# Input norms of the MLP and the conv folded into the norm that follows, squares of x summed later, small adds moved from GpSimd to VectorE

## The chip, the cores and the metric

The kernel runs on one core of a Trainium2 chip. The metric is the time of one execution in microseconds (us); the time of a version is the median of its runs. Engines are named as in the profile: PE is TensorE, DVE VectorE, ACT ScalarE, POOL GpSimd, SP SyncE.

## The reference

512 tokens of 1024 features pass through two layers of a first block, an mLSTM layer and a short-convolution layer, each followed by an MLP, and then through a second block (attention and a mixture of experts), which the change does not touch. Each mixer and each MLP stands between two RMS norms: one of its input, one of its output.

```python
def rms_norm(x, g):
    y = xf * lax.rsqrt(jnp.mean(xf * xf, axis=-1, keepdims=True) + EPS)
    return y * g

def short_conv_mixer(x, w_in, w_conv, w_out):
    bgate, cgate, xh = jnp.split(x @ w_in, 3, axis=-1)
    u = cgate * xh
    conv = lax.conv_general_dilated(u, w_conv[:, None, :], padding=[(CONV_WIDTH - 1, 0)],
                                    feature_group_count=D_MODEL, ...)
    return (bgate * conv) @ w_out

def sqrelu_mlp(x, w_up, w_down):
    h = jax.nn.relu(x @ w_up)
    return (h * h) @ w_down

for i in range(2):
    h = rms_norm(x, g[0])
    h = mlstm_mixer(h, ...) if i == 0 else short_conv_mixer(h, ...)
    x = x + rms_norm(h, g[1])
    h = sqrelu_mlp(rms_norm(x, g[2]), w_mlp_up[i], w_mlp_down[i])
    x = x + rms_norm(h, g[3])
```

Since relu is homogeneous, the factor rstd(x) of the norm in front of an MLP can be applied to the MLP's operand, to its hidden values (once, before the square) or to its output (as a square). In the conv it enters three times, once in each of bgate, cgate and xh.

## The kernel before

Everything is kept with features on the partitions and tokens along the free dimension, in eight feature tiles of 128 x 512 (`xres` is x). A float32 product is three matmuls on parts split into a high and a low part: `mm3` issues lines 92, 93 and 94. Weights come by DMA into `raw`; `wpiece` splits them: ACT casts the high part `wh` (line 85), another engine subtracts for the low part `wl` (line 86, on DVE unless `eng` says otherwise).

A layer ends in `boundary`. The last products of the layer come in four parts for each half of the tokens (256 each). `evac` takes them out of PSUM into `y` and gives their squares to `Sumsq.add` (ACT squares, line 194; the adds on line 196, on POOL except for the last two tiles). `colsum` sums these over the partitions by PE (line 207) and `rstd_cols` makes rstd(y) of it on DVE and ACT (lines 156 to 162); `bcast_rows` spreads it as a row over all partitions by PE transposes (line 216). Then `residual` handles feature tile after feature tile:

```python
nc.vector.scalar_tensor_tensor(t, self.y[k][:, sl], self.gpost(k), self.rb, ...)         # line 281
nc.vector.tensor_add(xk, xk, t)                                                          # 286: x += t
nc.scalar.activation(h, xk, AF.Copy, scale=self.gnext(k))                                # 288: high part
nc.vector.scalar_tensor_tensor(lo, xk, self.gnext(k), h.bitcast(F32), ...)               # 289: low part
nc.scalar.activation(self.sq[k][:, sl], xk, AF.Square)                                   # 292
```

`h` and `lo` are the operand (`op`) of the first products of the next layer, which `first` issues for the weight pieces w0 and w1, first with half 0 of the tokens, then with half 1. `squares` adds the squares of x (line 297, on POOL). A last column sum gives rstd(x), which the next layer gets as a function that makes rows of it (`rows`): the input norm is not applied to the operand, but to what comes out of the first products: in `mlp` at line 611 together with the relu, in `conv` at lines 713, 714 and 722. There are three such layer changes, mLSTM to MLP, MLP to conv, and conv to MLP; the second MLP ends in `boundary_out`, which feeds the attention instead.

`mlp` runs over eight blocks of 512 hidden features: up-products, `act` (relu, square, split), and `down`, whose results stay in `y`. At the first block they are copied there by ACT (line 660), later added by DVE (line 662), and the last block ends in the boundary. Between blocks a `filler` runs that prepares the second block's modulation vectors; its products on PE are line 816.

Each engine runs its instructions in the order in which they stand in its program; a scheduler in the building of the program moves some of them.

Of the kernel before, what the change touches and what calls it, by code (L numbers as in the profile page):

```python
# [18 lines left out]
S = 512  # L19
# [8 lines left out]
class Net:  # L28
# [123 lines left out]
    def rstd_cols(self, ms, w, scale):  # L152
        """(ms * scale + eps) ** -0.5 on [128, w]: a seed from a logarithm, one Newton step"""
# [21 lines left out]
    class Sumsq:  # L175
        """sums of squares over feature tiles, [128, S]"""
# [6 lines left out]
        def add(self, src, sl=slice(0, S)):  # L183
# [19 lines left out]
    def colsum(self, acc, d=D, n=4):  # L203
# [4 lines left out]
        return self.rstd_cols(pc[:, :n], n, 1.0 / d), pc  # L208
# [14 lines left out]
    def load_x(self, w):  # L223
        """x and the first weights, in the order of their use"""
# [10 lines left out]
    def start(self, first):  # L235
        """x feature-major, its split, first(k, operand) after each, then the statistics"""
# [19 lines left out]
    class Boundary:  # L256
        """The last products of one layer (mm(half, part), evac(half, part) for four parts finish y and ss) and the
        residual x += y * rstd(y) * gpost, one half of the tokens after the other."""

        def __init__(self, net, mm, evac, y, ss, gpost, gnext=None):  # L260
            self.net, self.mm, self.evac, self.y, self.ss, self.gpost, self.gnext = net, mm, evac, y, ss, gpost, gnext
            self.sq = [None] * KD
            self.ops = [(net.t([128, S], F32R, tag="op"), net.t([128, S], F32R, tag="op")) for _ in range(KD)] if gnext else None
            self.acc = net.t([128, S], tag="acc")
# [5 lines left out]
        def colsum(self, hf):  # L270
            self.c = self.net.colsum(self.ss.acc[:, self.net.HALF[hf]], n=2)
# [4 lines left out]
        def residual(self, hf, ks):  # L276
            net, nc = self.net, self.net.nc
            sl = net.HALF[hf]
            for k in ks:
# [5 lines left out]
                else:  # L285
# [20 lines left out]
    def boundary(self, mm, evac, y, ss, gpost, gnext, wnext):  # L306
        """... and the first products of the next layer; returns its operand, these products, a function for rows of rstd(x)"""
        b = self.Boundary(self, mm, evac, y, ss, gpost, gnext)
# [12 lines left out]
        w1 = self.wpiece(wnext[1], KD, 256, eng=self.nc.gpsimd)  # L321
# [3 lines left out]
        b.squares(0)  # L325
# [10 lines left out]
    def boundary_out(self, mm, evac, y, ss, gpost, fill):  # L336
        """... other products filling in; returns columns of rstd(x) for each half"""
        b = self.Boundary(self, mm, evac, y, ss, gpost)
# [29 lines left out]
    def mlstm(self):  # L368
# [87 lines left out]
        def stage_a(h):  # L456
            """what needs queries, keys and gates only"""
# [26 lines left out]
        def tokmajor(c0, act):  # L484
            """a token-major 256 column piece; act(chunk, psum)"""
# [83 lines left out]
    def out_proj(self, w, ops, gpost, gnext, wnext):  # L569
        """x += rmsnorm(w^T ops); returns the next operand"""  # L570
# [27 lines left out]
        return self.boundary(mm, evac, y, ss, gpost, gnext, wnext)  # L598

    def mlp(self, l, ops, pu0, rows, gpost, gnext, wnext, filler, fill=None):  # L600
# [8 lines left out]
        def act(u, src):  # L609
            t = self.t([128, S])  # L610
# [1093 lines left out]
```

## Time and profile before

| | |
|---|---|
| runs | 1860.73, 1858.69 and 1860.83 us; median 1860.73 |
| span of the profiled execution | 1854.4 us from the first to the last instruction |
| PE | 96% busy, mean granted clock 0.982 |
| DVE | 57% |
| ACT | 34% |
| POOL | 13% |
| DMA | 133 GB/s read from HBM, on average |

The profile was taken of one execution, and no time of its own is given for it beside the span: the median of the runs is 6.3 us longer than the span. The span ends at the last instruction that the profile shows. The granted clock is a share of TensorE's full speed of 2.4 GHz; 0.50 is the lower level of 1.2 GHz. A stretch with a share between the two has seen both.

### The profile page before, as it was taken

What the parts mean: (1) busy time and instruction counts of PE and PEld (TensorE: products, weight loads), DVE (VectorE), ACT (ScalarE), POOL (GpSimd) and SP (SyncE); (2) the same over time, 40 slices, a digit from 0 to 9 for tenths busy, and PEclk for the clock granted to TensorE, in tenths of its full rate; (3) what the DMA queues carried; (4) which work ended last, traced back from release to release, by engine and by line L of the source; (5) the groups of instructions that cost most, each with busy time, mean ns of one, the idle gap of its engine ahead of it and who ended that gap; (6) DMA issues with size and microseconds to landing.
All of it is one profiled execution on the core that took longest, in us unless ns stands there. A gap on an engine that the chain in (4) does not pass through costs nothing.

```text
span 1854.4 us, 24565 instructions
## 1 busy us (share of the span) xinstructions
PE 1774.5 (96%) x9877; PEld 1405.3 (76%) x9881; DVE 1059.3 (57%) x1935; ACT 635.0 (34%) x1150; POOL 238.8 (13%) x213
## 2 busy tenths in 40 slices
PE   7999999999999899999999999989989997999997
PEld 5799888888888888888888888888777886454534
DVE  4644674777765665746556445677777744132322
ACT  4444453222222432244322222344656633111112
POOL 1000140000000422222000001113233322000000
PEclk9999999999999899999999999989999998999999
DMA  6222423444542222532443332220100066799992
GB/s 191 69 69 69 159 69 114 133 133 134 178 141 97 72 69 93 162 109 92 136 136 95 102 103 91 69 73 12 24 13 16 13 202 226 257 387 386 387 373 103
DMA packets 191809, 248.19 MB, mean 134 GB/s; under 512 B 19783, under 2 KB 125648, under 8 KB 191568
## 3 DMA queue, kind: packets, MB, share of 16 engines
q1 hardware_dynamic: 188688, 244.70, 39.3%
q10 hardware_dynamic: 2656, 1.87, 0.3%
q8 instruction: 77, 1.26, 0.3%
q14 instruction: 36, 0.29, 0.1%
q0 software_dynamic: 352, 0.06, 0.0%
HBM read 244.52 MB, written 2.10 MB: 133 GB/s over the span
## 4 chain that ended last, share of the span: by engine, by line
PE 85%; DVE 9%; ACT 3%; issue 1%; POOL 1%; DMA 0%; SPq 0%; DVEq 0%; ACTq 0%; POOLq 0%
PE ps L92 21%; PE ps L93 20%; PE ps L94 20%; PE ps L1515 6%; PE ps L1489 3%; PE ps L1468 2%; PE ps L1115 2%; PE ps L1100 2%; DVE op L289 1%; DVE th L281 1%; DVE wl L86 1%; DVE xres L286 1%; PE pw L1243 1%; PE ps L1481 1%; PE ps L1482 1%
## 5 line engine op out<-in xcount | busy, mean ns | idle before, releaser
L93 PE MATMUL ps<-op,wh 128*128 128x512 f32 (+1 forms) x1808 | 663.8, 368 | 13.8 <-DVE op L289 13.1
L92 PE MATMUL ps<-op,wh 128*128 128x512 f32 (+1 forms) x1808 | 661.5, 370 | 8.4 <-ACT wh L85 2.9
L94 PE MATMUL ps<-op,wl 128*128 128x512 f32 (+1 forms) x1808 | 660.5, 367 | 0.0
L93 PEld LDWEIGHTS ps<-op,wh 128*128 128x128 f32 x1808 | 345.9, 192 | 75.9 <-DVE op L289 16.3
L92 PEld LDWEIGHTS ps<-op,wh 128*128 128x128 f32 x1808 | 343.3, 192 | 69.4 <-ACT op L288 4.1
L94 PEld LDWEIGHTS ps<-op,wl 128*128 128x128 f32 x1808 | 345.5, 191 | 59.2
L86 DVE TENSOR_TENSOR wl<-raw,wh 128x1024 fp32r<-128x1024 f32 x204 | 254.7, 1253 | 208.0 <-ACT wh L85 206.5
L85 ACT CAST wh<-raw 128x1024 fp32r<-128x1024 f32 x210 | 219.7, 1052 | 405.3 <-PE ps L93 284.6
L662 DVE TENSOR_TENSOR t<-t,ps 128x512 f32<-128x512 f32 x96 | 65.8, 686 | 110.1 <-PE ps L94 110.0
L1515 PE MATMUL ps<-mw,xs 128*64 128x512 f32 x400 | 107.1, 602 | 0.0
L811 DVE SCALAR_TENSOR_TENSOR u<-b,csilu,u 128x256 f32<-128x256 f32 x224 | 97.7, 479 | 4.4 <-DMA b<-in_w_mod_dram 3.5
L613 ACT ACTIVATE t<-t 128x512 f32<-128x512 f32 x64 | 40.3, 630 | 146.3 <-DVE t L611 146.0
L92 PE MATMUL ps<-wh,op 128*128 128x256 f32 x256 | 74.8, 293 | 0.1
L1499 DVE SCALAR_TENSOR_TENSOR ys<-ps,sm,ys 128x512 fp32r<-128x512 f32 x14 | 10.5, 749 | 110.0 <-ACT ys L1498 110.0
L93 PE MATMUL ps<-wl,op 128*128 128x256 f32 x256 | 72.0, 282 | 0.0
L94 PE MATMUL ps<-wh,op 128*128 128x256 f32 x256 | 71.5, 284 | 0.0
L611 DVE SCALAR_TENSOR_TENSOR t<-ps,rb 128x512 f32<-128x512 f32 x64 | 43.9, 688 | 47.7 <-PE ps L94 47.7
L1068 DVE TENSOR_REDUCE sm<-pw 128x1 f32<-128x768 f32 (+2 forms) x64 | 53.9, 854 | 30.0 <-PE pw L1243 17.4
L1515 PEld LDWEIGHTS ps<-mw,xs 128*64 128x64 f32 x400 | 31.3, 137 | 52.2 <-issue 49.9
L92 PEld LDWEIGHTS ps<-wh,op 128*128 128x128 f32 x256 | 48.2, 188 | 4.1 <-ACT og L507 2.3
L93 PEld LDWEIGHTS ps<-wl,op 128*128 128x128 f32 x256 | 48.3, 189 | 0.2
L94 PEld LDWEIGHTS ps<-wh,op 128*128 128x128 f32 x256 | 47.5, 188 | 0.1
(460 smaller groups left out, 2409.5 us busy)
## 6 DMA issues: line engine op xcount, KB each, us to landing
raw<-in_w_mlp_up_dram SPq DMA_DIRECT2D x32, 1024.0 KB, 5.4
raw<-in_w_mlp_down_dram SPq DMA_DIRECT2D x32, 1024.0 KB, 5.0
mw<-in_w_gate_dram SPq DMA_DIRECT2D x26, 1024.0 KB, 14.1
b<-in_w_mod_dram SPq DMA_DIRECT2D x48, 512.0 KB, 4.2
mw<-in_w_up_dram SPq DMA_DIRECT2D x24, 1024.0 KB, 14.2
mw<-in_w_down_dram SPq DMA_DIRECT2D x17, 1024.0 KB, 14.4
raw<-in_w_in_conv_dram SPq DMA_DIRECT2D x12, 1024.0 KB, 5.1
raw<-in_w_in_mlstm_dram SPq DMA_DIRECT2D x11, 1024.0 KB, 5.4
```

The costliest lines, as they stand in the source:

```text
L85: nc.scalar.copy(h, raw[:, k0:k0 + kk])
L86: (eng or nc.vector).tensor_sub(lo, raw[:, k0:k0 + kk], h.bitcast(F32))
L92: mm(out, st[0], mv[0], start=first, stop=False)
L93: mm(out, st[0], mv[1], start=False, stop=False)
L94: mm(out, st[1], mv[0], start=False, stop=last)
L611: nc.vector.scalar_tensor_tensor(t, src, 0.0, rb, op0=OP.max, op1=OP.mult)
L613: nc.scalar.activation(sq, t, AF.Square)
L662: nc.vector.tensor_add(y[i], y[i], p)
L811: nc.vector.scalar_tensor_tensor(acc[v], raw[:, k], c, acc[v], op0=OP.mult, op1=OP.add)
L1068: nc.vector.reduce_max(nm[e], p[e][:, 256:256 + n], axis=AX.X, negate=self.sink is None)
L1489: nc.tensor.matmul(py[e * 64:e * 64 + 64], aT[:, f, e * 64:e * 64 + 64], r[e][:, f], start=f == 0, stop=f == 3, tile_position=(0, e * 64))
L1515: nc.tensor.matmul(p[e * 64:e * 64 + 64], xs[:, k, s0:s0 + 64], r[e][:, k % 4], start=k == 0, stop=k == 7, tile_position=(0, e * 64))
```

## The change

It has five parts.

1. The rows of rstd(x) at the MLP's hidden values go. ACT computes the relu alone. What was left out is a factor per token; squared, it stands in y, so `factor` makes a column `f` and its multiple `f2` from rstd(x), and `colsum` with `fold` multiplies the mean square of y by it and rstd(y) by it. The conv leaves out one of its three factors in the same way and applies the other two at once, as the square `rb2`, on one product.
2. At the two ends of `out_proj`, where an MLP follows, `residual` computes no squares of x. `late_cols` does that in the MLP, in the code behind the first `down`, over whole tiles of 512 tokens, and ends in a column sum.
3. At the end of the first MLP the squares of x are still summed in the boundary, on DVE in place of POOL, in the code behind the first products of both halves.
4. The narrow adds (256 tokens) of `Sumsq` go from POOL to DVE, 28 in all, and so does the subtraction for w1 at the three layer changes, 2 instructions each.
5. The elementwise products of the conv go from POOL to DVE, with a copy of one factor by ACT.

```diff
@@ Sumsq.add
-            eng = nc.vector if i >= self.n - 2 else nc.gpsimd
+            eng = nc.vector if i >= self.n - 2 or lo + 2 != hi else nc.gpsimd
             eng.tensor_add(o, o, sq)
@@ colsum
+        f, f2 = fold
+        ms = self.sm([128, n])
+        nc.vector.tensor_mul(ms, pc[:, :n], f2)
+        cols = self.rstd_cols(ms, n, 1.0)
+        nc.vector.tensor_mul(cols, cols, f)
+        return cols, pc
+
+    def factor(self, cols, power):
+        v = self.nc.vector
+        f, f2 = cols, self.sm([128, 4])
+        if power == 2:
+            f = self.sm([128, 4])
+            v.tensor_mul(f, cols, cols)
+        v.scalar_tensor_tensor(f2, f, 1.0 / D, f, op0=OP.mult, op1=OP.mult)
+        return f, f2
@@ Boundary.residual, Boundary.squares
+                if self.sq is None:
+                    continue
...
-                (eng or self.net.nc.gpsimd).tensor_add(a, a, self.sq[k][:, self.net.HALF[hf]])
+                (eng or self.net.nc.vector).tensor_add(a, a, self.sq[k][:, self.net.HALF[hf]])
@@ boundary
-        w1 = self.wpiece(wnext[1], KD, 256, eng=self.nc.gpsimd)
+        w1 = self.wpiece(wnext[1], KD, 256)
         ps = [self.p() for _ in range(4)]
         b.first(w0, ps[0:2], 0)
         b.colsum(1)
-        b.squares(0)
         b.first(w1, ps[2:3], 0)
         b.bcast()
         b.first([(h[:, 128:], lo[:, 128:]) for h, lo in w1], ps[3:4], 0)
         b.residual(1, range(8))
-        b.squares(1)
         b.first(w0, ps[0:2], 1)
         b.first(w1, ps[2:4], 1)
+        if late:
+            return b.ops, ps, self.late_cols
+        b.squares(0)
+        b.squares(1)
         cols, _ = self.colsum(b.acc)
-        return b.ops, ps, lambda: self.bcast_rows(cols, 4, tag="rb")
+        return b.ops, ps, lambda: cols
+
+    def late_cols(self):
+        ss = self.Sumsq(self)
+        for k in range(KD):
+            ss.add(self.x[:, k])
+        return self.colsum(ss.acc)[0]
@@ mlp
-            nc.vector.scalar_tensor_tensor(t, src, 0.0, rb, op0=OP.max, op1=OP.mult)
+            nc.scalar.activation(t, src, AF.Relu)
...
-                pu = products(1, 0)
-                rb = rows()
                 acts(0, pu0)
-                acts(1, pu)
-                acts(1, products(1, 1))
+                for j in range(2):
+                    acts(1, products(1, j))
...
             o = down(f)
+            if f == 0:
+                fold = self.factor(cols(), 2)
@@ conv
+            cx = []
+            for hh in range(2):
+                t1 = self.t([128, S])
+                nc.scalar.copy(t1, pc[hh])
+                nc.vector.tensor_mul(t1, t1, px[hh])
+                cx.append(t1)
             if j == 0:
-                rb = rows()
+                fold = self.factor(cols(), 1)
+                c2 = self.sm([128, 4])
+                nc.vector.tensor_mul(c2, fold[0], fold[0])
+                rb2 = self.bcast_rows(c2, 4, tag="rb")
...
-                nc.vector.tensor_mul(t1, pc[hh], rb)
-                nc.vector.tensor_mul(t2, px[hh], rb)
-                nc.gpsimd.tensor_mul(u[:, 2:S + 2], t1, t2)
+                nc.vector.tensor_mul(u[:, 2:S + 2], cx[hh], rb2)
...
-                nc.vector.tensor_mul(bt, pb, rb)
-                nc.gpsimd.tensor_mul(yv, yv, bt)
+                nc.vector.tensor_mul(yv, yv, pb)
```

Lines that only move their number: in the changed kernel 281 is 301, 286 is 306, 288 is 308, 289 is 309, 297 is 319, 611 is 644, 613 is 646, 660 is 693, 816 is 852.

**POOL at the first layer change.** The name `acc351` holds the sum of squares of y, `acc403` that of x, `acc530` the later one of x in the MLP; `wl446` and `wl448` are the low parts of w1. From the last wide adds of the layer on, POOL's program before has:

```order
L196 TENSOR_TENSOR acc351_1975<-acc351_1975,th413_2296 128x256
L196 TENSOR_TENSOR acc351_1975<-acc351_1975,th419_2337 128x256
L86 TENSOR_TENSOR wl446_2469<-raw444_2466,wh445_2468 128x1024
L297 TENSOR_TENSOR acc403_2154<-acc403_2154,t427_2364 128x256
L297 TENSOR_TENSOR acc403_2154<-acc403_2154,t429_2371 128x256
L297 TENSOR_TENSOR acc403_2154<-acc403_2154,t433_2407 128x256
L297 TENSOR_TENSOR acc403_2154<-acc403_2154,t435_2414 128x256
L86 TENSOR_TENSOR wl448_2473<-raw444_2466,wh447_2472 128x1024
```

and now:

```order
L196 ISA
L196 TENSOR_TENSOR acc351_1975<-acc351_1975,t368_2100 128x512
L196 TENSOR_TENSOR acc351_1975<-acc351_1975,t370_2105 128x512
L196 TENSOR_TENSOR acc351_1975<-acc351_1975,t372_2110 128x512
L196 TENSOR_TENSOR acc530_3042<-acc530_3042,t531_3044 128x512
L196 TENSOR_TENSOR acc530_3042<-acc530_3042,t532_3047 128x512
L196 TENSOR_TENSOR acc530_3042<-acc530_3042,t533_3050 128x512
L196 TENSOR_TENSOR acc530_3042<-acc530_3042,t534_3053 128x512
L196 TENSOR_TENSOR acc530_3042<-acc530_3042,t535_3056 128x512
L753 MEMSET u1010_5870 128x2
```

Behind the three wide adds of the mLSTM's end all narrow adds, both subtractions and the adds of x's squares are gone, and the five wide adds of the MLP's late sum are POOL's next work.

**DVE at the first layer change, end of token half 0.** Here `th` are the products of line 281 (now 301) and `op` the low parts. Before:

```order
L196 TENSOR_TENSOR acc351_1975<-acc351_1975,th439_2448 128x256
L281 SCALAR_TENSOR_TENSOR th440_2452<-t385_2136,vc_115,ps414_2300 128x256
L281 SCALAR_TENSOR_TENSOR th442_2459<-t386_2137,vc_115,ps414_2300 128x256
L286 TENSOR_TENSOR xres_70<-xres_70,th440_2452 128x256
L289 SCALAR_TENSOR_TENSOR op398_2149<-xres_70,vc_115,op397_2148 128x256
L286 TENSOR_TENSOR xres_70<-xres_70,th442_2459 128x256
L289 SCALAR_TENSOR_TENSOR op400_2151<-xres_70,vc_115,op399_2150 128x256
L156 TENSOR_SCALAR sm454_2531<-ps453_2528 128x2
L289 SCALAR_TENSOR_TENSOR op402_2153<-xres_70,vc_115,op401_2152 128x256
```

and now:

```order
L196 TENSOR_TENSOR acc351_1975<-acc351_1975,th433_2436 128x256
L309 SCALAR_TENSOR_TENSOR op398_2149<-xres_70,vc_115,op397_2148 128x256
L301 SCALAR_TENSOR_TENSOR th434_2440<-t385_2136,vc_115,ps413_2299 128x256
L301 SCALAR_TENSOR_TENSOR th435_2445<-t386_2137,vc_115,ps413_2299 128x256
L306 TENSOR_TENSOR xres_70<-xres_70,th434_2440 128x256
L306 TENSOR_TENSOR xres_70<-xres_70,th435_2445 128x256
L86 TENSOR_TENSOR wl438_2453<-raw436_2450,wh437_2452 128x1024
L309 SCALAR_TENSOR_TENSOR op400_2151<-xres_70,vc_115,op399_2150 128x256
L86 TENSOR_TENSOR wl440_2457<-raw436_2450,wh439_2456 128x1024
L309 SCALAR_TENSOR_TENSOR op402_2153<-xres_70,vc_115,op401_2152 128x256
L156 TENSOR_SCALAR sm446_2515<-ps445_2512 128x2
```

The two subtractions for w1 stand ahead of the last two low parts, and the column sum's first step (line 156) stands behind all of them in place of ahead of the last.

**PE and ACT behind the first down block of the first MLP.** On PE `ps528` is the last product of that block now (`ps542` before). Before, the filler's products follow it:

```order
L92 MATMUL ps542_3086<-op491_2861,wh534_3037 128x512
L93 MATMUL ps542_3086<-op492_2862,wh534_3037 128x512
L94 MATMUL ps542_3086<-op491_2861,wl535_3038 128x512
L816 MATMUL ps549_3125<-ones_66,u545_3103 128x1 x2
L816 MATMUL ps549_3125<-ones_66,u546_3104 128x1 x2
```

and now the column sum of `acc530` stands between:

```order
L93 MATMUL ps528_3027<-op471_2743,wh520_2978 128x512
L94 MATMUL ps528_3027<-op470_2742,wl521_2979 128x512
L207 MATMUL ps538_3065<-ones_66,acc530_3042 128x1 x4
L852 MATMUL ps549_3107<-ones_66,u545_3085 128x1 x2
L852 MATMUL ps549_3107<-ones_66,u546_3086 128x1 x2
```

On ACT the copy of that last product was followed by the squares of the next hidden values (line 613):

```order
L85 CAST wh571_3237<-raw570_3235 128x1024
L85 CAST wh573_3241<-raw570_3235 128x1024
L660 COPY t543_3099<-ps542_3086 128x512
L613 ACTIVATE t565_3223<-t564_3221 128x512
L85 CAST wh586_3313<-raw585_3311 128x1024
```

and now by seven squares of x; the eighth, which opens `acc530`, stands much earlier:

```order
L85 CAST wh571_3219<-raw570_3217 128x1024
L85 CAST wh573_3223<-raw570_3217 128x1024
L693 COPY t529_3040<-ps528_3027 128x512
L194 ACTIVATE t531_3044<-xres_70 128x512
L194 ACTIVATE t532_3047<-xres_70 128x512
L194 ACTIVATE t533_3050<-xres_70 128x512
L194 ACTIVATE t534_3053<-xres_70 128x512
L194 ACTIVATE t535_3056<-xres_70 128x512
L194 ACTIVATE t536_3059<-xres_70 128x512
L194 ACTIVATE t537_3062<-xres_70 128x512
L158 ACTIVATE sm540_3071<-ps538_3065,eps_68 128x4
```

The last two of the eight tiles, `t536` and `t537`, are added by DVE; they stand behind two weight subtractions there.

## Rows read from the trace of the kernel before

**Rows 1.** The page: busy time and share of the span of each engine, and its instructions

```profile
PE 1774.5 (96%) x9877; PEld 1405.3 (76%) x9881; DVE 1059.3 (57%) x1935; ACT 635.0 (34%) x1150; POOL 238.8 (13%) x213
```

**Rows 2.** First layer change: length, busy PE PEld DVE ACT POOL, granted clock, DMA share, GB/s

```profile
248.00:252.00 4.00, 3.03 (x26) 2.82 (x24) 4.00 (x8) 3.26 (x9) 2.07 (x1) 1.00 0.79 248
252.00:256.00 4.00, 2.60 (x13) 2.40 (x14) 4.00 (x7) 2.13 (x7) 3.11 (x5) 0.71 0.01 4
256.00:260.00 4.00, 4.00 (x21) 4.00 (x20) 4.00 (x7) 1.93 (x5) 3.32 (x3) 0.50 0.00 0
260.00:264.00 4.00, 4.00 (x33) 3.90 (x32) 3.16 (x8) 1.97 (x6) 2.20 (x3) 0.94 0.70 262
268.00:280.00 12.00, 9.90 (x77) 9.08 (x77) 11.88 (x19) 6.77 (x15) 6.20 (x7) 1.00 0.01 1
```

**Rows 3.** The same over the whole of two other layer changes

```profile
828.00:860.00 32.00, 27.80 (x199) 26.42 (x198) 28.47 (x51) 17.25 (x39) 17.03 (x16) 0.89 0.17 58
632.00:668.00 36.00, 28.89 (x187) 26.79 (x188) 30.73 (x55) 17.73 (x40) 18.15 (x18) 0.81 0.16 51
```

**Rows 4.** DVE's timeline at the first layer change: start, duration, instruction

```profile
243.88 1.23 DVE L86 TENSOR_TENSOR wl<-raw,wh 128x1024 fp32r<-128x1024 f32 x1 [1.19 <-ACT wh L85]
245.02 0.47 DVE L281 SCALAR_TENSOR_TENSOR th<-t,vc,ps 128x256 f32<-128x256 f32 x1
...
250.40 2.17 DVE L289 SCALAR_TENSOR_TENSOR op<-xres,vc,op 128x256 fp32r<-128x256 f32 x1
...
256.92 0.41 DVE L196 TENSOR_TENSOR acc<-acc,th 128x256 f32<-128x256 f32 x1
257.25 0.86 DVE L281 SCALAR_TENSOR_TENSOR th<-t,vc,ps 128x256 f32<-128x256 f32 x2
258.04 1.80 DVE L286 TENSOR_TENSOR xres<-xres,th 128x256 f32<-128x256 f32 x1
...
261.92 0.47 DVE L289 SCALAR_TENSOR_TENSOR op<-xres,vc,op 128x256 fp32r<-128x256 f32 x1
...
265.20 0.87 DVE L281 SCALAR_TENSOR_TENSOR th<-t,vc,ps 128x256 f32<-128x256 f32 x2 [1.80 <-PE ps L216]
```

**Rows 5.** POOL's timeline at the first layer change

```profile
249.93 2.37 POOL L86 TENSOR_TENSOR wl<-raw,wh 128x1024 fp32r<-128x1024 f32 x1 [2.70 <-ACT wh L85]
...
257.06 2.49 POOL L86 TENSOR_TENSOR wl<-raw,wh 128x1024 fp32r<-128x1024 f32 x1 [0.68 <-ACT wh L85]
```

**Rows 6.** PE's timeline at the first layer change

```profile
252.63 0.38 PE L93 MATMUL ps<-op,wh 128*128 128x256 f32 x1 [1.60 <-DVE op L289]
...
282.34 0.95 PE L207 MATMUL ps<-ones,acc 128*128 128x1 f32 x8
```

**Rows 7.** DVE's timeline at the first MLP's end

```profile
626.73 2.90 DVE L86 TENSOR_TENSOR wl<-raw,wh 128x1024 fp32r<-128x1024 f32 x2
...
647.47 0.48 DVE L289 SCALAR_TENSOR_TENSOR op<-xres,vc,op 128x256 fp32r<-128x256 f32 x1 [0.18 <-ACT op L288]
```

**Rows 8.** PE's timeline at the second MLP's end

```profile
1227.68 1.02 PE L207 MATMUL ps<-ones,acc 128*128 128x1 f32 x4 [3.47 <-DVE acc L297]
```

**Rows 9.** The chain that ended last, at the start of the first MLP

```profile
294.64 0.44 PE ps L216 x4
```

**Rows 10.** The page, costliest groups: the square in the MLP

```profile
L613 ACT ACTIVATE t<-t 128x512 f32<-128x512 f32 x64 | 40.3, 630 | 146.3 <-DVE t L611 146.0
```

**Rows 11.** The timeline at the end of the first down block, all engines

```profile
328.42 0.40 PE L94 MATMUL ps<-op,wl 128*128 128x512 f32 x1
...
328.65 1.84 PE L816 MATMUL ps<-ones,u 128*128 128x1 f32 x16
...
329.57 0.58 ACT L660 COPY t<-ps 128x512 f32<-128x512 f32 x1
```

**Rows 12.** POOL's timeline ahead of the first layer change

```profile
226.37 4.04 POOL L196 TENSOR_TENSOR acc<-acc,t 128x512 f32<-128x512 f32 x3 [101.13 <-ACT t L194]
```

**Rows 13.** The instructions of line 196: shortest, median and longest duration in ns

```profile
L196 DVE TENSOR_TENSOR acc<-acc,t x2: 692/692/693, 1547.9 to 1554.3; 128x512 f32<-128x512 f32 x2
```

More of the change, by code (lines that the diff above doesn't have):

```diff
@@ L201, in rstd, with colsum @@
         return cols, self.bcast_rows(cols, n, copy, pc if n < 4 else None)
-    def colsum(self, acc, d=D, n=4):
+    def colsum(self, acc, d=D, n=4, fold=None):
         nc = self.nc
@@ L207, in colsum @@
             nc.tensor.matmul(pc[:, c:c + 1], acc[:, c * 128:(c + 1) * 128], self.ones, start=True, stop=True)
-        return self.rstd_cols(pc[:, :n], n, 1.0 / d), pc
+        if fold is None:
+            return self.rstd_cols(pc[:, :n], n, 1.0 / d), pc
+        f, f2 = fold
[12 more added lines that the diff above has]
+        return f, f2
     def bcast_rows(self, cols, n, copy=True, pb=None, tag="t"):
@@ L256, with __init__ @@
     class Boundary:
-        def __init__(self, net, mm, evac, y, ss, gpost, gnext=None):
+        def __init__(self, net, mm, evac, y, ss, gpost, gnext=None, fold=None, squares=True):
             self.net, self.mm, self.evac, self.y, self.ss, self.gpost, self.gnext = net, mm, evac, y, ss, gpost, gnext
-            self.sq = [None] * KD
+            self.fold = fold
+            self.sq = [None] * KD if squares else None
             self.ops = [(net.t([128, S], F32R, tag="op"), net.t([128, S], F32R, tag="op")) for _ in range(KD)] if gnext else None
-            self.acc = net.t([128, S], tag="acc")
+            self.acc = net.t([128, S], tag="acc") if squares else None
         def part(self, hf, i):
@@ L270, in colsum @@
         def colsum(self, hf):
-            self.c = self.net.colsum(self.ss.acc[:, self.net.HALF[hf]], n=2)
+            fold = self.fold and [f[:, 2 * hf:2 * hf + 2] for f in self.fold]
+            self.c = self.net.colsum(self.ss.acc[:, self.net.HALF[hf]], n=2, fold=fold)
         def bcast(self):
@@ L304, in first, with boundary @@
                                  k == 0, k == KD - 1)
-    def boundary(self, mm, evac, y, ss, gpost, gnext, wnext):
-        b = self.Boundary(self, mm, evac, y, ss, gpost, gnext)
+    def boundary(self, mm, evac, y, ss, gpost, gnext, wnext, fold=None, late=False):
+        b = self.Boundary(self, mm, evac, y, ss, gpost, gnext, fold, not late)
         for i in range(4):
@@ L567, in mlstm, with out_proj @@
         return hops
-    def out_proj(self, w, ops, gpost, gnext, wnext):
+    def out_proj(self, w, ops, gpost, gnext, wnext, fold=None):
         nc = self.nc
@@ L596, in evac, with mlp @@
             nc.scalar.copy(y[4 + i][:, sl], ph[hf, i][:, 0:256])
-        return self.boundary(mm, evac, y, ss, gpost, gnext, wnext)
-    def mlp(self, l, ops, pu0, rows, gpost, gnext, wnext, filler, fill=None):
+        return self.boundary(mm, evac, y, ss, gpost, gnext, wnext, fold, late=True)
+    def mlp(self, l, ops, pu0, cols, gpost, gnext, wnext, filler, fill=None):
         nc, a = self.nc, self.a
@@ L649, in down @@
                 if fill:
-                    return self.boundary_out(mm, evac, y, ss, gpost, fill)
-                return self.boundary(mm, evac, y, ss, gpost, gnext, wnext)
+                    return self.boundary_out(mm, evac, y, ss, gpost, fill, fold)
+                return self.boundary(mm, evac, y, ss, gpost, gnext, wnext, fold)
             for j in range(2):
@@ L679, in mlp, with conv @@
         return o
-    def conv(self, ops, pc0, rows):
+    def conv(self, ops, pc0, cols):
         nc, a = self.nc, self.a
@@ L720, in conv @@
                 nc.vector.scalar_tensor_tensor(yv, u[:, 2:S + 2], self.wconv(2, kk), yv, op0=OP.mult, op1=OP.add)
-                bt = self.t([128, S])
-                nc.vector.tensor_mul(bt, pb, rb)
-                nc.gpsimd.tensor_mul(yv, yv, bt)
+                nc.vector.tensor_mul(yv, yv, pb)
                 hops.append(self.split(yv, None))
-        return hops
+        return hops, fold
     def small_weights(self, src, k, n, pad, tag):
@@ L788, in block1 @@
         nx = self.mlp(0, *nx, g(0, 3), g(1, 0), [wc[:, D:D + 256], wc[:, 2 * D:2 * D + 256]], filler)
-        hops = self.conv(*nx)
-        nx = self.out_proj(a["w_out_conv"][0], hops, g(1, 1), g(1, 2), [wu[1][:, 0:256], wu[1][:, 256:512]])
+        hops, fold = self.conv(*nx)
+        nx = self.out_proj(a["w_out_conv"][0], hops, g(1, 1), g(1, 2), [wu[1][:, 0:256], wu[1][:, 256:512]], fold)
         return self.mlp(1, *nx, g(1, 3), None, [], filler, self.ctx_gemms())
```

6 lines of the change are left out of this document (2 added, 4 removed).

## The prediction

> **What bounds the kernel now.** I read the busy shares first: TensorE (PE) is busy 1774.5 of 1854.4 us, VectorE (DVE) 57%, GpSimd (POOL) 13% [rows 1]. So work taken from DVE, ACT or POOL is worth something only where PE waits for it. In the bodies of the two MLPs and of the conv PE does not wait, and time freed on POOL or DVE buys nothing there. PE idles at the layer changes, so I read those next, in stretches of a few us. The first one, mLSTM to MLP, begins with DVE's weight remainder at 243.88 [rows 4] and ends with PE's column sum of the squares of x at 282.34 [rows 6]. In three of its stretches PE is busy 3.03 of 4, 2.60 of 4 and 9.90 of 12 us: 4.5 us idle. Work around and behind the idle time runs at a lower granted clock, 0.71, 0.50 and 0.94: of the busy 2.60, 4.00 and 4.00 us, 0.75 + 2.0 + 0.24 = 3.0 us is lost to it [rows 2]. This layer change costs PE 7.5 us in all.
>
> Why PE idles shows on DVE and POOL. PE's wait of 1.60 us before its line 93 ends with DVE's L289, the low part of the next operand [rows 6]. L289 takes 0.47 us (261.92), the one at 250.40 took 2.17 [rows 4]: POOL's L86 ran from 249.93 for 2.37 [rows 5]. Under POOL's second L86 (257.06, 2.49) two L281, which read PSUM, took 0.86 together, at their usual pace, but the L286 behind them 1.80. POOL work on SBUF holds up the DVE instructions that feed PE.
>
> **The change part by part.** *mLSTM to first MLP, and conv to second MLP.* POOL's two L86, 4 narrow adds and 14 adds L297 leave the layer change. DVE gets the two L86 and the 4 adds; the squares of x leave the place altogether. From 243.88 to the last operand of token half 0 DVE then has, start to start, 4 L86 at 1.14 (243.88 to 245.02), 8 tiles at 0.39 + 0.34 + 0.39 = 1.12 (L281, L286, L289) and 3 adds at 0.33 (256.92 to 257.25): 4.6 + 9.0 + 1.0 = 14.6, with 0.4 for small waits 15.0. It ends at 258.9; now it ends at 261.92 + 0.47 = 262.4 [rows 4]. Half 1, which starts at 265.20 today, starts some 3.5 us earlier, while PE still has products of half 0 to do. Of the 7.5 us I let 1 stay, because DVE gives a tile per 1.12 us and the six matmuls on it take 0.7 (26 in 3.03 us [rows 2]). That is **-6.5**. The bounds are -7.5, all of it, and -3: the idle shrinks, but the clock falls anyway. At the other such place the instructions are the same, PE idles 32 - 27.8 = 4.2 us and loses 27.8 x 0.11 = 3.1 to the clock [rows 3], 7.3 in all: **-6.5** again. The two small multiplications of the fold hide in the wait for PE's transposes.
>
> *First MLP to conv.* Here 36 - 28.9 = 7.1 us are idle and 28.9 x 0.19 = 5.5 lost to the clock [rows 3], 12.6 in all. But DVE stays the slower engine: ahead of half 0's last operand stand 4 L86 (4.6), 8 tiles (9.0) and ten of the layer's PSUM adds and narrow adds (3.4), 17.0 from 626.73 on, which gives 643.7 where 647.47 + 0.48 = 648.0 is now [rows 7]. The 14 adds of squares now follow on DVE (4.8 us), and PE's column sum may wait for them. PE still waits some 5 us before half 0 is done, and the clock may fall as now. I take **-4**, near the shift of the last operand; bounds -8.6 and 0.
>
> *Second MLP to attention.* DVE had the squares' adds before. It gets 10 narrow adds (3.4 us) and the fold's multiplications ahead of the column sum, for which PE waited 3.47 us already [rows 8]. I take **+2**: a part of the 3.4 falls into waits that DVE has. Bounds -1 and +3.
>
> *Bodies of MLP and conv.* The row broadcast of the first norm goes: four transposes, 0.44 us, in each MLP [rows 9], **-0.9**. The Relu moves to ACT, where the square (L613, 630 ns) already stood behind the casts of weights [rows 10], and DVE loses the multiplication L611. I cost it at 0, covered by PE's queue of products; without that cover a block would lose about such an instruction, 0.6 us.
>
> *Squares late.* In each MLP PE's column sum now stands directly behind the last product of the first down block, with nothing of PE between. On ACT seven squares stand behind the copy of that product. Today this copy starts at 329.57 and takes 0.58 [rows 11], so the first of them ends at 330.15 + 0.63 = 330.8. POOL then adds five 128x512 tiles one after the other, at 4.04 / 3 = 1.35 each [rows 12], 6.75, to 337.5; the squares, 0.63 each, keep ahead of it. DVE adds the last two at 0.69 [rows 13]: 338.9. PE's last product starts at 328.42 and today the next work follows at 328.65 [rows 11]. So PE stands still 10.3 us, twice: **+20.6**. The bounds are 8.8 each (the chain starts 1.5 us sooner, copy and first square being done early) and 12 (adds slowed by DVE's L86 beside them). The columns are not used before the layer's end; it is only the column sum's place in PE's queue that makes PE wait.
>
> A rule of the Trainium skill speaks of the last bound: "SBUF — State Buffer", section "SBUF: two separate sides", says that DVE instructions with two SBUF inputs and GpSimd instructions that read SBUF hold a shared pair of ports alone, each for its whole length. The pair of 2.17 and 2.37 us in rows 4 and 5 agrees. By it, as an estimate, one or two L86 take turns with the adds, +1.2 to +2.4 us a stall.
>
> PE idle for less than this was followed by the low clock at the first layer change, at a loss of 3.0 us [rows 2]. I take that twice: **+6**. Bounds 0 (no such long wait inside an MLP is in the trace) and 11 (twice 5.5, as at the first MLP's end).
>
> Sum: -6.5 - 6.5 - 4 + 2 - 0.9 + 20.6 + 6 = +10.7 on the span of 1854.4, which gives 1865.1. The median of the runs, 1860.73 (1858.69 to 1860.83), is 6.3 above that span, so the time is **1871.4 us**.
>
> **The rivals.** *The late squares don't hold PE* (0.08). That needs squares that run before the last copy, so that POOL's last add ends before about 329. For it: ACT and POOL have time to spare in the down block. Against it: the order of the instructions on ACT and PE. Without stall and clock the sum is -15.9: 1844.8, faster.
> *The layer changes give back nearly all* (0.14): -7.5 - 7.5 - 8.6 - 1 - 0.9 = -25.5 against +26.6: 1861.8, no change. For it: all the POOL work that slows DVE goes. Against it: DVE's 1.12 a tile stays above PE's 0.7.
> *They give back little* (0.13): -3 - 3 + 0 + 3 - 0.9 = -3.9 against +26.6: 1883.4. For it: an idle of 0.97 us of 4 was enough for the clock to be lower in the stretch behind [rows 2].
> *The Relu holds up PE* (0.05): a Relu that stands behind a waiting cast frees its PSUM late. One us in each of 16 blocks gives 1887.4. Against it: the square stood there without PE waiting.
>
> **How the numbers follow.** The forecast case has 0.60; its own range is 1862 to 1878, from the bounds of the stall, half of those of the clock and of the layer changes. The range to be given leans to the second rival, whose result is nearer than the third's: 1858 to 1880. A measurement tells 0.2%, 3.7 us, from no change: slower is above 1864.5, faster below 1857.0. Slower has most of 0.60 and the 0.18 of the last two rivals, 0.73; no change has the second rival and the low end of the forecast, less its own low end, 0.15; faster has the first rival and that low end, 0.12.
>
> **What would show it.** In both MLPs a column sum (L207) with an idle time of about 10 us before it that ends with DVE's add, POOL's five adds back to back before that, and a clock near 0.5 for about 6 us behind. At the first layer change every L289 at 0.47 and no clock below 1; the last one's column sum later by some 2 us. I am wrong if PE has other work across the 10 us, or if the first layer change still idles over 3 us.

## The result, and the profile after

The changed kernel takes 1868.17 us (median of four runs, 1866.6 to 1871.3), the kernel before, measured beside it, 1859.71. The ratio is 1.0053 with a 95% interval of 1.0041 to 1.0065: slower by 7.6 to 12.1 us. The forecast was 1871.4, slower, with a range of 1858 to 1880.

The profiled execution spans 1867.7 us, 13.3 more than the one of before. To see where they arise I put rows of PE's timeline side by side that stand at the same place in both programs (start, duration, line). In the kernel before:

```profile
240.85 0.50 PE L207 MATMUL ps<-ones,acc 128*128 128x1 f32 x4
...
375.42 1.84 PE L816 MATMUL ps<-ones,u 128*128 128x1 f32 x16
...
622.57 0.50 PE L207 MATMUL ps<-ones,acc 128*128 128x1 f32 x4
...
819.64 0.50 PE L207 MATMUL ps<-ones,acc 128*128 128x1 f32 x4
...
907.32 0.95 PE L816 MATMUL ps<-ones,u 128*128 128x1 f32 x8
...
953.19 0.95 PE L816 MATMUL ps<-ones,u 128*128 128x1 f32 x8
...
1197.94 0.50 PE L207 MATMUL ps<-ones,acc 128*128 128x1 f32 x4
...
1267.97 0.50 PE L207 MATMUL ps<-ones,t 128*128 128x1 f32 x4
```

and in the changed kernel, where the number in brackets is PE's idle time ahead and what ended it:

```profile
244.39 0.50 PE L207 MATMUL ps<-ones,acc 128*128 128x1 f32 x4
...
334.40 1.87 PE L207 MATMUL ps<-ones,acc 128*128 128x1 f32 x8 [10.40 <-DVE acc L196]
...
386.47 1.73 PE L852 MATMUL ps<-ones,u 128*128 128x1 f32 x15
...
633.62 0.50 PE L207 MATMUL ps<-ones,acc 128*128 128x1 f32 x4
...
821.59 0.50 PE L207 MATMUL ps<-ones,acc 128*128 128x1 f32 x4
...
911.48 1.87 PE L207 MATMUL ps<-ones,acc 128*128 128x1 f32 x8 [10.39 <-DVE acc L196]
...
962.51 0.95 PE L852 MATMUL ps<-ones,u 128*128 128x1 f32 x8
...
1206.92 0.50 PE L207 MATMUL ps<-ones,acc 128*128 128x1 f32 x4
...
1279.47 0.50 PE L207 MATMUL ps<-ones,t 128*128 128x1 f32 x4
```

Subtracting one start from the next gives the length of a stretch. PE finished the first down block at 328.65 before, where its next work starts [rows 11], and at 334.40 - 10.40 = 324.00 now, where its last product ends; these two marks lie 0.2 us apart, which moves 0.2 between the first row of the table and the second, and likewise in the second MLP. Each row of this table is a stretch between two such places:

| stretch | before | changed | difference | forecast |
|---|---|---|---|---|
| first layer change, to the end of the first MLP's first down block | 87.80 | 79.61 | -8.2 | -7.0 |
| from there to the end of the next down block | 46.77 | 62.47 | +15.7 | +13.3 |
| first MLP to conv, and the conv | 197.07 | 187.97 | -9.1 | -4 |
| conv to second MLP, to the end of its first down block | 87.68 | 79.50 | -8.2 | -7.0 |
| from there to the end of the next | 45.87 | 61.42 | +15.6 | +13.3 |
| second MLP to attention | 70.03 | 72.55 | +2.5 | +2 |

They sum to +8.3. Of the other 5 us -0.3 stand in the bodies of the MLPs, and the rest lies where the program is the same: the mLSTM stage, unchanged but for two narrow adds at its end, ended 3.5 us later in this execution (240.85 against 244.39), and 1.8 us come behind 1279.47. That the 3.5 us are not the change's shows in another run below: the one with all late adds on DVE is the same program as the changed kernel up to these adds, and there the stage ends at 240.46. The last section takes this up.

The stall stands in the changed kernel as the forecast put it. Its timeline around the end of the first down block, all engines:

```profile
323.61 0.39 PE L94 MATMUL ps<-op,wl 128*128 128x512 f32 x1
323.80 1.04 ACT L85 CAST wh<-raw 128x1024 fp32r<-128x1024 f32 x1 [0.35 <-PE ps L93]
323.98 2.35 DVE L86 TENSOR_TENSOR wl<-raw,wh 128x1024 fp32r<-128x1024 f32 x2
324.76 0.58 ACT L693 COPY t<-ps 128x512 f32<-128x512 f32 x1
325.23 3.75 ACT L194 ACTIVATE t<-xres 128x512 f32<-128x512 f32 x7
325.94 6.88 POOL L196 TENSOR_TENSOR acc<-acc,t 128x512 f32<-128x512 f32 x5 [92.01 <-ACT t L194]
...
332.85 1.49 DVE L196 TENSOR_TENSOR acc<-acc,t 128x512 f32<-128x512 f32 x2 [6.52 <-POOL acc L196]
...
334.40 1.87 PE L207 MATMUL ps<-ones,acc 128*128 128x1 f32 x8 [10.40 <-DVE acc L196]
```

PE's last product, the copy, the squares, POOL's five adds (6.88, forecast 6.75) and DVE's two (1.49) follow each other, and PE waits for the end of it. Behind the stall the clock is low. The columns are length, busy time of PE, PEld, DVE, ACT and POOL, granted clock, DMA share and GB/s:

```profile
328.00:332.00 4.00, 0.00 (x0) 0.00 (x0) 0.00 (x0) 0.98 (x2) 3.77 (x4) 0.50 0.72 239
332.00:336.00 4.00, 1.60 (x8) 1.60 (x8) 1.39 (x2) 0.00 (x0) 0.82 (x1) 0.50 0.01 2
336.00:340.00 4.00, 4.00 (x19) 4.00 (x19) 0.61 (x4) 0.47 (x2) 0.00 (x0) 0.50 0.00 0
340.00:344.00 4.00, 4.00 (x11) 3.08 (x11) 4.00 (x16) 0.00 (x0) 0.00 (x0) 0.54 0.00 0
344.00:348.00 4.00, 4.00 (x18) 3.21 (x18) 4.00 (x11) 0.60 (x1) 0.00 (x0) 1.00 0.51 154
```

Of the busy 1.60, 4.00 and 4.00 us in the second, third and fourth stretch 0.8 + 2.0 + 1.8 = 4.6 is lost to it. The first layer change shows the other side. In these two stretches, which answer to [rows 2] and to the second row of [rows 3], PE is busy 31.54 of 32 us at full clock where it was idle for 4.5, and at the first MLP's end the idle time falls from 7.1 to 2.1 of 36 us, the clock from 0.81 up to 0.95:

```profile
252.00:284.00 32.00, 31.54 (x235) 29.62 (x234) 28.06 (x63) 18.38 (x35) 0.00 (x0) 1.00 0.30 100
...
644.00:680.00 36.00, 33.94 (x233) 31.43 (x233) 32.00 (x82) 19.06 (x44) 0.00 (x0) 0.95 0.30 98
```

DVE at the end of half 0 of the first layer change, answering to [rows 4], has every L309 (then L289) at 0.48:

```profile
259.25 1.22 DVE L86 TENSOR_TENSOR wl<-raw,wh 128x1024 fp32r<-128x1024 f32 x1
260.38 0.48 DVE L309 SCALAR_TENSOR_TENSOR op<-xres,vc,op 128x256 fp32r<-128x256 f32 x1
260.78 1.22 DVE L86 TENSOR_TENSOR wl<-raw,wh 128x1024 fp32r<-128x1024 f32 x1
261.92 0.48 DVE L309 SCALAR_TENSOR_TENSOR op<-xres,vc,op 128x256 fp32r<-128x256 f32 x1
```

From its first L86 (247.42) to the end of the last one here (262.40) it takes 15.0 us, the forecast's number, where it took 18.5.

### The profile page after: what moved, and what is told of

It is laid out like the page before. It is cut to its first block, busy times and chain, and to the rows that moved or that the text cites. A ratio compares the mean times of both kernels' runs of the same rounds, so it can differ in the third digit from the quotient of the medians.

```text
span 1867.7 us, 24499 instructions
## 1 busy us (share of the span) xinstructions
PE 1778.3 (95%) x9869; PEld 1408.9 (75%) x9873; DVE 1010.0 (54%) x1941; ACT 672.8 (36%) x1204; POOL 151.9 (8%) x131
## 4 chain that ended last, share of the span: by engine, by line
PE 87%; DVE 6%; ACT 3%; issue 2%; POOL 1%; DMA 0%; SPq 0%; DVEq 0%; ACTq 0%; POOLq 0%
PE ps L92 21%; PE ps L93 21%; PE ps L94 21%; PE ps L1551 6%; PE ps L1525 3%; PE ps L1151 2%; PE ps L1504 2%; PE ps L1136 2%; PE pw L1279 1%; PE ps L852 1%; PE ps L1517 1%; ACT wh L85 1%; PE ps L1518 1%; POOL acc L196 1%; PE pw L1278 1%
## 5 line engine op out<-in xcount | busy, mean ns | idle before, releaser
L86 DVE TENSOR_TENSOR wl<-raw,wh 128x1024 fp32r<-128x1024 f32 x210 | 258.9, 1236 | 277.2 <-ACT wh L85 276.6
L847 DVE SCALAR_TENSOR_TENSOR u<-b,csilu,u 128x256 f32<-128x256 f32 x224 | 96.4, 479 | 4.2 <-DMA b<-in_w_mod_dram 3.6
L644 ACT ACTIVATE t<-ps 128x512 f32<-128x512 f32 x64 | 38.0, 594 | 137.0 <-PE ps L94 137.0
L196 POOL TENSOR_TENSOR acc<-acc,t 128x512 f32<-128x512 f32 x21 | 28.1, 1338 | 415.1 <-ACT t L194 414.2
L648 DVE CAST op<-t 128x512 fp32r<-128x512 f32 x64 | 27.1, 424 | 53.2 <-ACT t L646 39.5
L92 PEld LDWEIGHTS ps<-wh,op 128*128 128x128 f32 x256 | 48.5, 190 | 4.1 <-ACT og L539 2.3
```

The costliest lines, as they stand in the source:

```text
L86: (eng or nc.vector).tensor_sub(lo, raw[:, k0:k0 + kk], h.bitcast(F32))
L92: mm(out, st[0], mv[0], start=first, stop=False)
L644: nc.scalar.activation(t, src, AF.Relu)
L847: nc.vector.scalar_tensor_tensor(acc[v], raw[:, k], c, acc[v], op0=OP.mult, op1=OP.add)
```

## The experiments

Times are medians; each is compared with runs of the kernel before on the same chip (1859.1, 1858.6 and 1859.1 us in the three groups).

**Where the column sum stands in PE's queue.** Squares and adds are left where they are; only the column sum, and what follows it, moves behind the next down block.

```diff
             if f == 0:
-                fold = self.factor(cols(), 2)
+                late = cols()
+            if f == 1:
+                fold = self.factor(self.colsum(late)[0], 2)
@@ late_cols
-        return self.colsum(ss.acc)[0]
+        return ss.acc
```

> The changed kernel with the late column sum one down block later in PE's queue; squares and adds stay where they are. Theory (only its place in PE's queue makes PE wait): both idle times of 10.4 us and the low clock behind them go, 2 x (10.4 + 4.5) = 29.8 us less than the changed kernel's 1868.2, 1838.4 us. Rival (the squares and adds themselves hold up the next block, because the next Relu on ACT stands behind seven squares): an idle time of some 4 us moves to the next products, with the clock loss, 2 x 8 us remain, 1854 us.

Measured: 1840.13 us, ratio 0.9899 (0.9884 to 0.9913). The stretch behind the first down block takes 47.57 us in place of 62.47. This is 0.8 more than before the change, the column sum itself, and it begins without idle time in front of it:

```profile
369.99 0.39 PE L94 MATMUL ps<-op,wl 128*128 128x512 f32 x1
370.22 0.95 PE L207 MATMUL ps<-ones,acc 128*128 128x1 f32 x8
```

So it was the column sum's place in PE's queue that made PE stand still: the same squares and adds now run beside the products, and no wait of PE shows. The rival's 4 us at the next products don't show.

**The length of the chain.** All seven late adds on DVE.

```diff
@@ Sumsq.add (which gets an argument eng=None)
-            eng = nc.vector if i >= self.n - 2 or lo + 2 != hi else nc.gpsimd
+            eng = eng or (nc.vector if i >= self.n - 2 or lo + 2 != hi else nc.gpsimd)
@@ late_cols
-            ss.add(self.x[:, k])
+            ss.add(self.x[:, k], eng=self.nc.vector)
```

> The changed kernel with all seven late adds on DVE. Theory (the chain of adds sets the length of the stall): the first square ends 0.6 us after its start, seven adds at 0.65 us make 4.6 in place of POOL's 6.9 plus DVE's 1.5, so each idle time is 3.9 us shorter, 6.5 in place of 10.4; the clock falls as before; 1868.2 - 7.8 = 1860.4 us. Rival (ACT's squares set it): seven squares in 3.75 us end the same, at most 1 us off each stall beyond that, and if the wait is some other work of POOL nothing changes, 1868 us.

Measured: 1862.57 us, ratio 1.0021 (1.0011 to 1.0031), 5.6 us less than the changed kernel. The timeline of this run:

```profile
321.30 3.75 ACT L194 ACTIVATE t<-xres 128x512 f32<-128x512 f32 x7
322.31 3.87 DVE L196 TENSOR_TENSOR acc<-acc,t 128x512 f32<-128x512 f32 x5
...
326.63 1.49 DVE L196 TENSOR_TENSOR acc<-acc,t 128x512 f32<-128x512 f32 x2 [0.46 <-DVE acc L196]
...
328.18 1.86 PE L207 MATMUL ps<-ones,acc 128*128 128x1 f32 x8 [8.11 <-DVE acc L196]
```

The idle time is 8.11 and, in the second MLP, 7.75 in place of 10.4: 2.3 and 2.6 less, where I had expected 3.9. I had mis-sized three things. An add takes some 0.76 us (3.87 for five, 1.49 for two) and not 0.65; each one needs the result of the last, and where other work follows an add instead, as with the column sum moved back, it starts 0.60 us behind it (334.39 to 334.99). DVE comes to the adds only at 322.31, behind two L86. And 0.46 us lie between the fifth and the sixth. The direction holds: a shorter chain made a shorter stall.

**The squares of x in the boundary.** No late squares; they are summed on DVE behind the first products, as the change does it at the first MLP's end.

```diff
-        return self.boundary(mm, evac, y, ss, gpost, gnext, wnext, fold, late=True)
+        return self.boundary(mm, evac, y, ss, gpost, gnext, wnext, fold)
```

> The changed kernel without the late squares: at the ends of out_proj the squares of x are summed in the boundary as at the first MLP's end, on DVE behind the first products. Theory (with POOL out of the way DVE has room for them): no stall in the MLP, 29.8 us less than the changed kernel, and 14 adds at 0.34 lie beside PE's products of half 1; 1838 to 1841 us. Rival (the boundary's column sum then waits for DVE, as the last layer change's does): some 3 us idle and a clock loss of 3 in two places, 1850 us.

Measured: 1838.82 us, ratio 0.9889 (0.9874 to 0.9904). The first layer change takes 80.21 us, 0.6 more than with the late squares, which is less than the column sum of 0.8 that stands in it again; the stretch behind takes 46.76, as in the kernel before. At a layer change the late squares save nothing, and as they stand they cost 15.7 us behind it.

**Which of the moves brings the gain.** From the kernel before, one or two kinds of work are moved from POOL to DVE, without the fold: w1's subtraction alone; w1 and the narrow adds; squares and narrow adds; all three; w1 and squares.

```diff
# w1
-        w1 = self.wpiece(wnext[1], KD, 256, eng=self.nc.gpsimd)
+        w1 = self.wpiece(wnext[1], KD, 256)
# narrow adds
-            eng = nc.vector if i >= self.n - 2 else nc.gpsimd
+            eng = nc.vector if i >= self.n - 2 or lo + 2 != hi else nc.gpsimd
# squares of x
-                (eng or self.net.nc.gpsimd).tensor_add(a, a, self.sq[k][:, self.net.HALF[hf]])
+                (eng or self.net.nc.vector).tensor_add(a, a, self.sq[k][:, self.net.HALF[hf]])
...
-        b.squares(0)
...
-        b.squares(1)
         b.first(w0, ps[0:2], 1)
         b.first(w1, ps[2:4], 1)
+        b.squares(0)
+        b.squares(1)
```

> The kernel before with one edit, the subtraction for w1 from POOL to DVE (6 instructions). Theory (all POOL work on SBUF slows DVE, the adds of squares included): per layer change DVE saves the two long waits, 1.7 + 1.4, and pays 2 x 1.14, 0.8 us less; the L289 beside POOL's adds stay at 0.95; PE's idle time falls by 1 to 3 us a place and the clock may fall still: 1860 - 6 = 1854 us. Rival (the two subtractions alone were the cause): the first three layer changes give back nearly what the change gave back, 25 us together, 1835 us.

> The kernel before with w1 and the narrow adds on DVE, squares' adds on POOL at their old places. Theory (the squares' adds on POOL beside DVE are the larger part of the cause): little more than with w1 alone (1854.8): 1853 us. Rival (the narrow adds count, since the column sum of y hangs on them): 1846 us.

> The kernel before with the squares' adds and the narrow adds on DVE, in the places that they have in the changed kernel; the subtraction for w1 stays on POOL, no fold. Theory (both the subtractions and the adds on POOL slow DVE): the two long waits of 1.7 and 1.4 us per layer change stay, PE idles some 2 us a place and the clock may fall, so of the 21 us between the kernel before and the one with everything moved a half is left: 1850 us. Rival (the adds of the squares were the whole cause): 1840 us.

> The kernel before with all three kinds of work moved from POOL to DVE (w1, narrow adds, squares behind the first products), no fold, no late squares. Theory (the moves bring the gain, the fold only the transposes of two row broadcasts, 0.9 us): 1838.8 + 1 = 1840 us. Rival (the fold frees DVE, 64 x 0.69 us and more in the conv, and that is needed to make room): 1846 us or more.

> The kernel before with w1 and the squares' adds on DVE, the narrow adds of the squares of y left on POOL. Theory (DVE's time at the layer changes is what counts, and the narrow adds cost it more than they free: moving them beside w1 alone lost 2.9 us): 1836.9 - 2.9 = 1834 us. Rival (each narrow add on POOL slows a DVE instruction beside it, and the pairs L86 and narrow add come back): 1840 us.

| moved to DVE | us | ratio (95%) | first layer change | first MLP's end and conv |
|---|---|---|---|---|
| nothing | 1859.71 | | 87.80 | 197.07 |
| w1 | 1854.83 | 0.9970 (0.9957 to 0.9984) | 88.19 | 194.52 |
| w1, narrow adds | 1857.68 | 0.9995 (0.9983 to 1.0007) | 87.02 | 196.53 |
| squares, narrow adds | 1848.13 | 0.9942 (0.9923 to 0.9961) | 84.45 | 191.59 |
| all three | 1836.89 | 0.9884 (0.9865 to 0.9902) | 80.65 | 187.92 |
| w1, squares | 1834.75 | 0.9865 (0.9850 to 0.9880) | 80.17 | 187.91 |

The last two columns are stretches of the profiled execution, taken as above. The squares are worth most: 20 us once w1 has moved (1854.83 to 1834.75). w1 is worth another 11 once squares and narrow adds have moved (1848.13 to 1836.89), and 4 by itself or 1 together with the narrow adds while the squares are on POOL. The narrow adds gain nothing; in both pairs that differ by them alone the run that has them on DVE is the slower, by 2.9 and 2.1 us, at the edge of the intervals or inside them. With w1 alone on DVE the squares' adds start sooner on POOL and sit beside the residual instead, as this timeline shows:

```profile
251.61 2.91 POOL L297 TENSOR_TENSOR acc<-acc,t 128x256 f32<-128x256 f32 x3 [3.41 <-ACT t L292]
...
252.10 0.96 DVE L289 SCALAR_TENSOR_TENSOR op<-xres,vc,op 128x256 fp32r<-128x256 f32 x1
...
252.98 0.95 DVE L286 TENSOR_TENSOR xres<-xres,th 128x256 f32<-128x256 f32 x1
...
261.73 0.61 PE L207 MATMUL ps<-ones,acc 128*128 128x1 f32 x4 [1.29 <-POOL acc L297]
```

L289 and L286 take twice their time beside three adds, and PE waits for a POOL add itself. With the squares and narrow adds moved and w1 left on POOL, the two subtractions run back to back and hold two DVE instructions, each for as long as one of them, and PE behind them:

```profile
253.15 4.87 POOL L86 TENSOR_TENSOR wl<-raw,wh 128x1024 fp32r<-128x1024 f32 x2 [19.30 <-ACT wh L85]
...
253.63 2.17 DVE L289 SCALAR_TENSOR_TENSOR op<-xres,vc,op 128x256 fp32r<-128x256 f32 x1
...
255.73 2.58 DVE L286 TENSOR_TENSOR xres<-xres,th 128x256 f32<-128x256 f32 x1
...
255.86 0.39 PE L93 MATMUL ps<-op,wh 128*128 128x256 f32 x1 [1.43 <-DVE op L289]
...
258.75 0.44 PE L93 MATMUL ps<-op,wh 128*128 128x256 f32 x1 [1.92 <-DVE op L289]
```

With all three moved PE is busy 30.98 of 32 us there and the clock stays full:

```profile
248.00:280.00 32.00, 30.98 (x250) 30.03 (x249) 31.38 (x74) 19.51 (x45) 0.00 (x0) 1.00 0.27 86
```

The rival by which the subtractions alone were the cause falls, and so does the one by which the squares alone were it: with w1 left on POOL 11 of 22 us are missing. One rival stands untested. The squares' adds changed their place in the program together with their engine, from between the first products to behind them, and no run has them on POOL in the new place; how the gain divides between engine and place is not shown. What the timelines show for the engine is L289 and L286 at 0.96 and 0.95 us beside POOL's adds, in place of 0.48 and 0.42. I had expected 1850 for squares and narrow adds, where 1848.13 was measured, and 1853 for w1 and narrow adds, where it was 1857.68.

**The fold alone.** The changed kernel with POOL's work back on POOL at its old places and no late squares: what is left of the change is the fold, the Relu on ACT and the conv's products on DVE.

> The fold alone: Relu on ACT, one row less in each MLP, the conv's products on DVE, while w1, the narrow adds and the squares of x stay on POOL at their old places and no squares are late. Theory (bodies of MLP and conv are PE's, so only two transposes groups of 0.44 us go): within 1 us of the kernel before, 1858 us. Rival (the fold shortens the chains at the layer changes or the conv): 1853 us or less.

Measured: 1858.16 us, ratio 0.9993 (0.9984 to 1.0002): no change that can be told. The run with everything moved and no fold (1836.89) and the one with the fold (the squares in the boundary, 1838.82) agree with that.

**The last layer change.** The narrow adds of the second MLP's end go back to POOL, once with the fold and the squares in the boundary, once without the fold.

```diff
@@ Sumsq
-        def __init__(self, net, n=8):
-            self.net, self.n = net, n
+        def __init__(self, net, n=8, narrow=None):
+            self.net, self.n, self.narrow = net, n, narrow or net.nc.vector
@@ Sumsq.add
-            eng = nc.vector if i >= self.n - 2 or lo + 2 != hi else nc.gpsimd
+            eng = nc.vector if i >= self.n - 2 else nc.gpsimd if lo + 2 == hi else self.narrow
@@ mlp
-        ss = self.Sumsq(self)
+        ss = self.Sumsq(self, narrow=nc.gpsimd if fill else None)
```

> The run with the squares in the boundary, with the narrow adds of the second MLP's end back on POOL (10 instructions). Theory (they are what stands ahead of the last layer change's column sum): the 2.5 us that it lost come back, 1838.8 - 2.5 = 1836.3 us. Rival (the wait there is set by DVE's adds of squares of x, or POOL's adds slow DVE as much as they take off it): 1838.8 us, no change.

> All moved and no fold, with only the second MLP's narrow adds back on POOL. Theory (as with the fold, where the last layer change got 2.0 us shorter): 1836.9 - 2 = 1834.9 us. Rival (that difference was the chance of the clock): 1836.9 us.

Measured: 1837.22 us, ratio 0.9888 (0.9868 to 0.9907), against 1838.82, and 1834.34, ratio 0.9872 (0.9855 to 0.9889), against 1836.89. In the profiles the last layer change takes 68.96 against 70.93 and 70.13 against 70.36. Both medians are lower, by 1.6 and 2.6 us, but the intervals overlap widely. This stays unclear.

The versions from 1834 to 1840 us all beat both kernels, by 1.0 to 1.35% against the kernel before; most of them the runs don't tell apart. The one with the lowest ratio, w1 and squares on DVE without the fold (interval up to 0.9880), is just clear of the one with the column sum moved back (from 0.9884).

## Why the prediction was right, point by point

**What bounds the kernel.** Right: the work that the fold takes from DVE and POOL in the bodies of MLP and conv bought nothing that can be told (the fold alone, 0.9993), and the gains that the stretches show lie in the layer changes.

**mLSTM to MLP and conv to MLP, -6.5 each.** Right in mechanism and nearly in size: -8.2 each in the profile, of which 0.45 is the transposes, booked apart, and 0.8 the column sum, which moved to the stall. That leaves -7.0. DVE's 15.0 us up to the last operand came out exactly. The cause was not told finely enough: the prediction showed POOL's subtractions as what slows DVE, while the runs show that the adds of squares, in their old place on POOL, count for more.

**First MLP to conv, -4.** Mis-sized, and outside its bounds (the lower one, -8.6, was given without working): -9.1, and the same with the moves alone and no fold (187.92 against 197.07). DVE's work up to half 0's last operand was forecast as 17.0 us and took 637.78 to 654.91, 17.1. The step that failed was the one behind it, "PE still waits some 5 us before half 0 is done, and the clock may fall as now". I took the gain to be near the shift of the last operand. PE waits not for the last operand but for each one as it comes; with L309 at 0.48 throughout it waited 0.31 and 1.53 us for two operands and 0.21 for a weight, all in half 0 and none in half 1, and the low clock, which had cost 5.5 us, cost 1.7 (33.94 x 0.05).

**Second MLP to attention, +2.** The profile has +2.5, but three runs with the same instructions there have 71.50, 70.18 and 70.93 in place of 72.55, +1.5, +0.2 and +0.9 over before. The sign fits, the size is not settled, and the step was another one: PE waited 0.92, 0.30 and 3.47 us for the three column sums there and now waits 0.36, 1.81 and 2.97. That is 0.5 more in all, and not at the last one, where the prediction put it; the other 2.0 us are PE busy for longer, at a lower clock in parts.

**Row broadcast, -0.9, and the Relu on ACT, 0.** Within what the fold alone allows: with it the stretches up to the first down block are 0.46 and 0.32 us shorter than before (87.34 and 87.36). The rival by which the Relu holds up PE, at 16 us more, is out.

**Squares late, +20.6.** Right: 10.40 and 10.39 us, both ended by DVE's add behind POOL's five, and shown to be the queue's order by moving only the column sum.

**The clock behind them, +6.** Mis-sized: each stretch is 15.7 and 15.6 longer, 10.4 of it the idle time, 0.8 the column sum that moved there and 4.5 the clock, +9 in all.

**The sum and the base.** The sum was 10.7 and the stretches give 8.3, 2.4 less. That it came so near is in part luck: the conv's gain was put 5.1 us too small and the clock's cost 3 us too small, and the two errors offset each other. The base was in effect the median of before, 1860.73, since the span and the 6.3 us above it add up to that; measured beside the changed kernel this median is 1859.71, 1.0 lower. The two together, 3.4, account for the 3.2 us by which the forecast lies above 1868.17. The 6.3 us do not all lie outside the span, which did the forecast no harm: in the later runs of the kernel before 1.7 to 3.1 us lie outside it, and two executions with the same span of 1854.4 took 1856.49 and 1857.47. The rest is that the profiled execution of before was a fast one, by some 3 to 4 us. This goes with spans that differ by 13.3 where the medians differ by 8.5.

**The rule on the ports.** The Trainium skill, "SBUF — State Buffer", section "SBUF: two separate sides", lets whichever of the two engines starts first hold the shared ports for its whole instruction, while the other waits. The 2.17 and 2.58 us of L289 and L286 under POOL's two subtractions (4.87) agree with it. The extra 1.2 to 2.4 us a stall that the prediction worked out by it did not come: DVE's last L86 ended 0.4 us after POOL's first add began, and DVE was idle for 6.52 us from there on.

## What to carry to other kernels

Work that nobody waits for still costs time when its last step stands in the queue of the engine that bounds the kernel: move that step back until its inputs are long done, before looking at the work itself. At a place where one engine feeds the bounding one, count what other engines do to it, too: in the kernel before POOL's adds of squares took 0.87 us each at the first layer change, and no wait of PE there ended with one. Yet moving them and six subtractions to the busier DVE, with the adds placed behind the first products, gave 22 to 24 us. When a change has several parts, run its parts: here one gained 22 us, one lost 28 or 29, and one did nothing that can be told.

## What was not expected of the hardware

The granted clock fell or stayed high after the same wait of the same program. In the mLSTM stage, which the versions have in common, PE waits 1.81 or 1.82 us at about 72 us. The stretch that holds it reads, in the kernel before, in the changed kernel, in the run with all three moved and in the one with all late adds on DVE:

```profile
70.00:80.00 10.00, 7.94 (x50) 5.88 (x50) 6.85 (x12) 3.89 (x9) 0.00 (x0) 1.00 0.35 104
```

```profile
70.00:80.00 10.00, 7.72 (x26) 4.52 (x26) 6.66 (x11) 4.04 (x8) 0.00 (x0) 0.70 0.34 101
```

```profile
70.00:80.00 10.00, 7.93 (x33) 5.35 (x33) 7.61 (x13) 4.44 (x8) 0.00 (x0) 0.83 0.28 87
```

```profile
70.00:80.00 10.00, 8.19 (x51) 5.93 (x50) 6.47 (x11) 3.79 (x8) 0.00 (x0) 1.00 0.36 105
```

Clock 1.00, 0.70, 0.83 and 1.00; the second and the fourth are the same program up to here. Over the profiles the first column sum behind this stage starts between 240.46 and 246.16 us, whatever was changed. So a difference of 3 us between two profiles of this kernel can be that alone, and stretches between fixed places tell more than spans. It also means that one row, like those from which the prediction took its cost of 3.0 us a stall and its third rival, does not tell what the clock does behind the same idle time in the next execution.

POOL is slowed by DVE as well. With the column sum moved back, DVE has the filler's work beside POOL's five adds:

```profile
325.57 7.82 POOL L196 TENSOR_TENSOR acc<-acc,t 128x512 f32<-128x512 f32 x5 [92.01 <-ACT t L194]
...
326.55 2.76 DVE L847 TENSOR_SCALAR u<-b,csilu 128x256 f32<-128x256 f32 x2
...
329.24 5.23 DVE L849 SCALAR_TENSOR_TENSOR u<-b,csilu,u 128x256 f32<-128x256 f32 x5
```

The five adds take 7.82 us where they took 6.88 with DVE idle beside them but for the first 0.4 us, and DVE's two L847 take 2.76 where the same two (L845 there) took 0.61 in the changed kernel, though each has a single tile as input beside a column.
